# Compressing four samples' caches ahead, and two pairs of samples' attention beside the prompt's

## The chip, the core and the metric

The kernel runs on one core of a Trainium2 chip. Five engines with queues of their own work side by side: TensorE (PE) does the matrix products, VectorE (DVE), ScalarE (ACT) and GpSimd (POOL) the elementwise work, SyncE (SP) starts transfers. Each engine takes its instructions strictly in the order of its queue; an instruction whose inputs are not ready holds up everything behind it on that engine. GpSimd also starts transfers: the gathers, which fetch rows named by a list of indices. The metric is the device time of one execution, 3109.91 us before (median of 3 runs, 3104.84 to 3112.84 us).

## What is computed

One inference step of a two-layer decoder for a prompt of 512 tokens and 8 samples of one token each, in fp32. Every layer is a half-step SwiGLU, a mixer of three branches (an S5 state space, the attention NSA, a short convolution), and another half-step SwiGLU. The change is inside NSA. For a sample with 2048 earlier tokens, NSA does three things with its cache:

```python
def nsa_compress(x_raw, pe, w1, w2):      # 2048 cached rows -> 127 compressed keys and values
    ...
    h = jax.nn.gelu(h_a[:, :-1] + h_b[:, 1:] + h_pe)
    return h @ w2

# nsa_core, cut: kc, vc are the compressed keys and values
p_c = masked_softmax(s_c, ...)            # s_c = q . kc
o_c = p_c @ vc                            # branch 1: compressed
imp = p_c.sum(3) @ cmp_to_sel_map         # which blocks of 64 rows matter
score, idx = ...top_k(imp, 16)            # branch 2: the 16 best blocks
o_s = softmax(q . ks_sel) @ vs_sel
o_w = softmax(q . kw) @ vw                # branch 3: the last 512 rows
o = g[...,0]*o_c + g[...,1]*o_s + g[...,2]*o_w
```

A sample's attention therefore needs its compressed keys and values first. The prompt has the same three branches over its own 512 tokens, and does not depend on the samples.

## The kernel before

Every fp32 product of the layers' weights is three products of split operands (L239 to L241). These fill most of the time; the change touches the stretch between them in which `mid(l)` does the samples' compression and the attention. It is passed once in each layer, around 494 to 767 us and around 2000 to 2306 us of the span.

- **Compression of one sample** (`compress_cache`, L708 the products, 96 of them; `second`, L730 to L740, a gelu on ScalarE, six small products and the elementwise ends that make `kcT` and `vc`). Its raw pages come over SP's queue (L641) into `cx` (even samples, one buffer) or `raw` (odd samples, two buffers). It is a generator that yields `None` after each sample, so `upto(C, 2)` runs it two samples further.
- **Attention of a pair of samples** (`samples(l, g)`, g = 0 to 3, called S0 to S3 here): compressed scores L1138, the choice of blocks, scores of the selected pages L1189, of the window L1198, values of the pages L1249 and of the window L1258, compressed values L1264, and the end L1273. All eight pages of each half are multiplied and masked, so `sg` holds whole pages: of the 32 pages of a pair 12 come by gathers which GpSimd starts (L1118) and 20 by SP (L1122). Pair g+1 is asked for in the code right after the values of pair g (its `sag` pool holds one pair only), and the window rows `W` follow (L1127).
- **The prompt's attention** (`prompt_attention`, a generator of heads, three branches in each of four tiles of 128 tokens). A head is two scores (L1048 to L1050), a maximum on VectorE (L1051), an exponential on ScalarE (L1052), transposes (L1060), their copies, and values (L1072). After the fourth head of a branch come a reciprocal (L1077), a multiply that spreads the gates over the heads (L1079, on GpSimd, its result is `over`), a product of `over` that brings it into a score bank (L1098, the "correction" below), and the multiply and add of L1101 to L1103 (the add on GpSimd).

`weave` takes steps from several generators by their estimated cost in ns; that fixes the order of the program, from which a scheduler makes the order of each engine's queue. Before, two samples are compressed alone; S0, S1 and S2 are woven each with the compression of two further samples; S3 is woven with the prompt's attention, whose remaining heads then run alone. While S3 lives, the prompt's values have one bank (`paY`), afterwards two (`last`).

Of the kernel before, what the change touches and what calls it, by code (L numbers as in the profile page):

```python
# [122 lines left out]
class Trunk:  # L123
# [376 lines left out]
    def mid(self, l):  # L500
        nc, I = self.nc, self.I
        right, att = self.right, ExitStack()
        keep = self.pool(right, "keepb", side="right")
        self.ysam = keep.tile([128, 4, NS], F32, name="ysam")
        a = self.pool(att, "att", side="right")
        self.rows = a.tile([128, 4, 512], F32, name="rows")
        self.srows = a.tile([NS, 512], F32, name="srows")
        self.qT = a.tile([128, 4, 512], F32, name="qT")
        self.ks = a.tile([128, 2, 2, 512], F32R, name="ks")
        self.kTs = a.tile([128, 2, NS], F32, name="kTs")  # L510
        self.QB = a.tile([128, NS, 32], F32, name="QB")
        self.gtok = a.tile([128, 4, 24], F32, name="gtok")
        self.gat = a.tile([128, 4, 3], F32, name="gat")
        self.kcp = a.tile([128, 2, 32], F32, name="kcp")
        self.vcp = a.tile([128, 4, 2, 64], F32, name="vcp")
        self.w2 = a.tile([128, 2, 64], F32, name="w2")
        self.w2r = a.tile([128, 64], F32, name="w2r")
        self.hpe = a.tile([128, 2], F32, name="hpe")
        kcv, sag = self.pool(att, "kcv", 2, side="right"), self.pool(att, "sag", 4, side="right")
        sw = self.pool(att, "sw", 2, side="right")  # L520
        self.sgq = []
        sb = ExitStack()
        self.open_banks(4, 2)
        self.saT = self.psum(sb, "saT", 2, "right")
        cxs = ExitStack()
        with ExitStack() as sf, ExitStack() as sc:
            cx, G = self.project_kvq(l, cxs, sc, self.pool(sf, "ft", 4, side="right"), sag, sw)
        self.banks.close()
        self.saM, self.saS = (self.psum(sb, n, k, "right") for n, k in (("saM", 1), ("saS", 2)))
        with ExitStack() as sc, ExitStack() as pb:  # L530
            self.cacc, self.ctp = self.psum(pb, "cacc", 2), self.psum(pb, "ctp", 1)
            cp = self.pool(sc, "cmp")
            with ExitStack() as s0:
                C = self.compress_cache(l, cp, kcv, cx, G, self.compress_start(l, self.pool(s0, "cp")))
                self.finish(self.upto(C, 2))
            sa = self.pool(att, "sa", side="right")
            S = [self.samples(l, g, sa, sag, sw) for g in range(4)]
            for g in range(3):
                self.weave(self.slow(S[g]), self.upto(C, 2))
        cxs.close()  # L540
        ybs = ExitStack()
        self.yb = self.pool(ybs, "yb").tile([128, 4, 512], F32, name="yb")
        with ExitStack() as sc, ExitStack() as pb:
            self.paS, self.paY = self.psum(pb, "paS", 2), self.psum(pb, "paY", 1)
            self.score_banks, self.value_banks = [self.paS, self.saS], [self.paY]
            self.weave(self.last(S[3]), self.prompt_attention(l, self.pool(sc, "pa", 3)))
        att.close()
        sb.close()
        self.open_banks(4, 4)
        kc = self.pool(right, "keepc", side="right")  # L550
        self.yc = [kc.tile([128, 4, NTOK], F32R, name=f"yc{i}") for i in range(2)]
        ybh, ybl = (kc.tile([128, 4, NTOK], F32R, name=n) for n in ("ybh", "ybl"))
        for src, g, c in [(self.ysam, slice(0, 4), slice(0, NS))] + \
                [(self.yb[:, g:g + 1], slice(g, g + 1), slice(NS, NTOK)) for g in range(4)]:
            nc.scalar.activation(ybh[:, g, c], src, AF.Copy)
            nc.vector.tensor_sub(ybl[:, g, c], src, ybh[:, g, c].bitcast(F32))
        ybs.close()
        mg1, mg2 = self.pool(right, "mg1", side="right"), self.pool(right, "mg2", 2, side="right")
        left = ExitStack()
        self.ya = self.pool(left, "keepya").tile([128, 4, NTOK], F32, name="ya")  # L560
        sc, sr = ExitStack(), ExitStack()
        s5 = self.s5(l, self.pool(sc, "s5"), self.pool(sc, "s52", 2))
        conv = self.conv(l, self.pool(sr, "cv"), self.pool(sr, "cv2", 2), self.pool(sr, "cw", 2))
        merge = self.merge(l, mg1, mg2, (ybh, ybl))
        over = []

        def first():
            yield from s5
            yield from self.until(lambda: over)
            sc.close()  # L570
            kg = self.pool(right, "keepa", side="right")
            self.yg = [kg.tile([128, 4, NTOK], F32R, name=f"yg{i}") for i in range(2)]
            yield from self.glu(l, self.pool(left, "glu"), self.pool(left, "glu2", 2))

        def second():
            yield from conv
            sr.close()
            over.append(True)
            yield from self.upto(merge, 1)

        self.weave(first(), second())
        left.close()
        self.open_banks()
        mg = self.pool(right, "mg", side="right")
        self.mh = mg.tile([128, KD, NTOK], F32R, name="mh")
        self.ml = mg.tile([128, KD, NTOK], F32R, name="ml")
        self.open_res()
        for k in range(KD):
            for a, b in HALF:
                nc.gpsimd.tensor_add(self.xf[:, k, a:b], self.xh[:, k, a:b].bitcast(F32), self.xl[:, k, a:b].bitcast(F32))  # L590
        self.finish(merge)
        self.set_next(self.pairs(I["w_o"][l], 4))
        self.project_out(l, self.mh, self.ml, self.ffn_tiles(I["ffn2_w_gu"][l]))
        right.close()
# [69 lines left out]
    def compress_cache(self, l, p, kcv, cx, G, start):  # L664
# [47 lines left out]
        def second(b, acc):  # L712
            if b % 2 == 0:
                self.kcT = kcv.tile([128, 2, 128], F32, name="kcT")
                self.vc = kcv.tile([128, 2, 128], F32, name="vc")
            kcT, vc = self.kcT[:, b % 2], self.vc[:, b % 2]
            h = p.tile([128, 4, 128], F32, name="hc")
            nc.vector.memset(h[:, :, 127:128], 0.0)
# [13 lines left out]
            pa = self.bank(self.ctp)  # L732
# [30 lines left out]
        for b in range(NS):  # L763
            acc = [self.bank(self.cacc) for _ in range(1 if b else 2)]
            if b + 1 < NS:
                N = self.fetch_cmp(l, b + 1, cx)
            for s in range(8):
                if s < 7:
                    prepare(b, G, s + 1)
                elif b + 1 < NS:  # L770
                    G = N
                    prepare(b + 1, G, 0)
                products(b, acc, s)
                yield 1720.0
            yield from second(b, acc)
            yield None
# [353 lines left out]
    def samples(self, l, g, p, pg, pw):  # L1130

        nc = self.nc
        G = self.sgq[g]
        QB, kcT, vc = self.QB, self.kcT, self.vc
        M = self.bank(self.saM)

        for j in range(2):
# [48 lines left out]
        for c in range(2):  # L1186
            S = self.bank(self.saS)
# [6 lines left out]
        S = self.bank(self.saS)  # L1194
# [760 lines left out]
```

## Time and profile before

| quantity | value |
|---|---|
| median of 3 runs | 3109.91 us (3104.84 to 3112.84) |
| the profiled execution | 3104.94 us |
| its span | 3103.2 us |
| TensorE busy | 98% |
| GpSimd busy | 17% |
| granted clock of TensorE over the span | 0.987 |
| S2 beside the compression of two samples, layer 0 and 1 | 45.6 and 42.9 us |
| S3 beside the prompt's attention, layer 0 and 1 | 48.4 and 48.4 us |

The span leaves out 1.7 us around it. A share of busy time is a mean over all stages: a wait is looked for in the stretch in which it stands, and there the row's idle time before an instruction names what ended it. The granted clock is the share of TensorE's full 2.4 GHz that was allowed; 0.5 is its lower level of 1.2 GHz.

### The profile page before, as it was taken

Reading aid. Unit: us, or ns where it says so; the run is one execution under the profiler, and the core shown is the slowest. Engines: PE = TensorE matmul, PEld = TensorE weight load, DVE = VectorE, ACT = ScalarE, POOL = GpSimd, SP = SyncE. Lnnn points to the kernel's source line nnn. Section 1 sums busy time; section 2 is a strip of 40 time slices with the busy share of each in tenths; the row PEclk is TensorE's granted clock in tenths of the full one; section 3 lists DMA queues with packets and bytes.
Section 4 is the critical chain, followed back from the end, with each engine's and each line's share of the span. In section 5 each row is a group of like instructions: output and inputs, shape, how many; then the busy total and the mean of one; then the engine's idle time right before and its main releaser. Section 6 shows DMA issues by size and latency. Waiting matters only on the chain. (4 is left out here: it accounts for less than half of the span.)

```text
span 3103.2 us, 62136 instructions
## 1 busy us (share of the span) xinstructions
PE 3028.1 (98%) x25364; PEld 2906.8 (94%) x25364; DVE 1598.7 (52%) x3586; ACT 1120.1 (36%) x2226; POOL 536.1 (17%) x809
## 2 busy tenths in 40 slices
PE   8999999999999999999999999999999999999998
PEld 8999998777999999999999999887789999999998
DVE  7633356566655365333496333565666453743334
ACT  4332235456224233232233222354652242333322
POOL 2611031321001021001147010213210010210010
PEclk9999999999999999999999999999999999999999
DMA  5543254632553232232234332547234433223221
GB/s 159 198 148 133 89 159 134 209 96 63 156 138 103 88 101 91 82 99 86 82 121 169 96 103 76 172 124 218 83 93 140 122 98 102 89 82 103 89 87 64
DMA packets 358630, 360.17 MB, mean 116 GB/s; under 512 B 40068, under 2 KB 341668, under 8 KB 358216
## 3 DMA queue, kind: packets, MB, share of 16 engines
q1 hardware_dynamic: 342584, 333.58, 34.4%
q0 software_dynamic: 7440, 20.00, 2.2%
q8 instruction: 199, 3.26, 0.4%
q10 hardware_dynamic: 8320, 2.62, 0.4%
q14 instruction: 87, 0.71, 0.1%
HBM read 332.48 MB, written 36.28 MB: 119 GB/s over the span
## 5 line engine op out<-in xcount | busy, mean ns | idle before, releaser
L239 PE MATMUL ps<-xh,whi 128*128 128x264 f32 (+1 forms) x4448 | 1257.6, 285 | 14.1 <-ACT whi L228 6.1
L240 PE MATMUL ps<-xl,whi 128*128 128x264 f32 (+1 forms) x4448 | 1257.4, 284 | 2.0 <-DVE xl L323 2.0
L241 PE MATMUL ps<-xh,wlo 128*128 128x264 f32 (+1 forms) x4448 | 1254.1, 283 | 2.4 <-DVE wlo L229 2.4
L229 DVE TENSOR_TENSOR wlo<-raw,whi 128x1024 fp32r<-128x1024 f32 (+3 forms) x432 | 496.0, 1151 | 741.2 <-ACT whi L228 736.9
L239 PEld LDWEIGHTS ps<-xh,whi 128*128 128x128 f32 x4448 | 837.2, 189 | 18.7 <-ACT whi L228 6.9
L240 PEld LDWEIGHTS ps<-xl,whi 128*128 128x128 f32 x4448 | 839.5, 189 | 3.5 <-DVE xl L323 2.2
L241 PEld LDWEIGHTS ps<-xh,wlo 128*128 128x128 f32 x4448 | 838.5, 189 | 4.1 <-DVE wlo L229 3.6
L228 ACT ACTIVATE whi<-raw 128x1024 fp32r<-128x1024 f32 (+2 forms) x452 | 444.6, 988 | 891.0 <-PE ps L240 776.4
L240 PE MATMUL ps<-hl,whi 128*128 128x256 f32 (+1 forms) x1408 | 398.3, 283 | 0.0
L239 PE MATMUL ps<-hh,whi 128*128 128x256 f32 (+1 forms) x1408 | 398.2, 283 | 0.0
L241 PE MATMUL ps<-hh,wlo 128*128 128x256 f32 (+1 forms) x1408 | 398.1, 283 | 0.0
L241 PEld LDWEIGHTS ps<-hh,wlo 128*128 128x128 f32 x1408 | 265.3, 188 | 0.2
L239 PEld LDWEIGHTS ps<-hh,whi 128*128 128x128 f32 x1408 | 264.9, 188 | 0.3
L240 PEld LDWEIGHTS ps<-hl,whi 128*128 128x128 f32 x1408 | 264.8, 188 | 0.1
L260 POOL TENSOR_TENSOR xf<-xf,shift 128x264 f32<-128x264 f32 (+1 forms) x84 | 79.4, 983 | 1028.6 <-ACT shift L257 1028.6
L384 DVE TENSOR_TENSOR s<-s,ps 128x264 f32<-128x264 f32 (+1 forms) x176 | 74.3, 424 | 277.3 <-PE ps L241 277.0
L708 PE MATMUL ps<-xc,whi 128*128 128x256 f32 (+1 forms) x1024 | 167.4, 297 | 1.0 <-ACT xc L693 0.9
L385 ACT ACTIVATE hh<-s 128x264 fp32r<-128x264 f32 (+1 forms) x176 | 72.7, 415 | 245.2 <-DVE s L384 245.1
L708 PEld LDWEIGHTS ps<-xc,whi 128*128 128x128 f32 x1024 | 142.2, 193 | 14.6 <-issue 7.7
L1118 POOL DMA_INDIRECT sg<-in_selT_dram,idx x96 | 96.2, 1002 | 275.9 <-PE ps L1249 248.7
L382 ACT ACTIVATE s<-ps 128x264 f32<-128x264 f32 (+1 forms) x176 | 66.3, 379 | 128.7 <-PE ps L241 126.5
L386 DVE TENSOR_TENSOR hl<-s,hh 128x264 fp32r<-128x264 f32 (+1 forms) x176 | 76.5, 436 | 33.5 <-ACT hh L385 33.5
(471 smaller groups left out, 4206.8 us busy)
## 6 DMA issues: line engine op xcount, KB each, us to landing
raw<-in_ffn_w_gu_dram SPq DMA_DIRECT2D x86, 1024.0 KB, 5.3
raw<-in_w_in_dram SPq DMA_DIRECT2D x38, 1024.0 KB, 5.4
raw<-in_ffn_w_down_dram SPq DMA_DIRECT2D x32, 1024.0 KB, 4.9
sg<-in_selT_dram SPq DMA_DIRECT2D x160, 128.0 KB, 3.1
cx<-in_cmpT_dram SPq DMA_DIRECT2D x128, 128.0 KB, 2.2
raw<-in_cmpT_dram SPq DMA_DIRECT2D x128, 128.0 KB, 2.5
raw<-in_ffn_w_down_dram SPq DMA_DIRECT2D x16, 768.0 KB, 4.3
W<-in_winT_dram SPq DMA_DIRECT2D x16, 512.0 KB
```

Source lines behind the costliest of these rows:

```text
L228: self.copy = self.nc.scalar.activation(hi, raw, AF.Copy)
L229: self.lo.tensor_sub(lo, raw, hi.bitcast(F32))
L239: nc.tensor.matmul(o, hi[:, k], rh, start=start and k == 0, stop=False)
L240: nc.tensor.matmul(o, hi[:, k], rl, start=False, stop=False)
L241: nc.tensor.matmul(o, lo[:, k], rh, start=False, stop=stop and k == nk - 1)
L260: nc.gpsimd.tensor_sub(self.xf[:, g, a:b], self.xf[:, g, a:b], sc[:, :n])
L382: nc.scalar.activation(s[:, :n], g, AF.Silu)
L384: nc.vector.tensor_mul(s[:, :n], s[:, :n], u)
L385: nc.scalar.activation(hh[:, j, a:b], s[:, :n], AF.Copy)
L386: nc.vector.tensor_sub(hl[:, j, a:b], s[:, :n], hh[:, j, a:b].bitcast(F32))
L708: nc.tensor.matmul(o, w[:, 2 * qq + q2, :], x[:, 2 * q2:2 * q2 + 2, z:z + n], start=not b and s < 2 and q2 + z + m == 0, stop=s > 5 and q2 ...
L1118: nc.gpsimd.indirect_dma_start(out=t[:, k], out_offset=None, in_=flat, in_offset=bass.IndirectOffsetOnAxis(ap=self.idx[:, l, b, z, k:k + 1 ...
```

## The change

Four samples are compressed alone. S0 and S1 are woven each with two further samples. S2 and S3, one after the other, are woven with the prompt's attention. So that compressed keys and values can be kept longer, their pool gets a third buffer, and each pair's are kept in a list from which `samples` takes its own.

```diff
--- before.py
+++ after.py
@@ -516,9 +516,9 @@
         self.w2 = a.tile([128, 2, 64], F32, name="w2")
         self.w2r = a.tile([128, 64], F32, name="w2r")
         self.hpe = a.tile([128, 2], F32, name="hpe")
-        kcv, sag = self.pool(att, "kcv", 2, side="right"), self.pool(att, "sag", 4, side="right")
+        kcv, sag = self.pool(att, "kcv", 3, side="right"), self.pool(att, "sag", 4, side="right")
         sw = self.pool(att, "sw", 2, side="right")
-        self.sgq = []
+        self.sgq, self.kcq = [], []
         sb = ExitStack()
         self.open_banks(4, 2)
         self.saT = self.psum(sb, "saT", 2, "right")
@@ -532,10 +532,10 @@
             cp = self.pool(sc, "cmp")
             with ExitStack() as s0:
                 C = self.compress_cache(l, cp, kcv, cx, G, self.compress_start(l, self.pool(s0, "cp")))
-                self.finish(self.upto(C, 2))
+                self.finish(self.upto(C, 4))
             sa = self.pool(att, "sa", side="right")
             S = [self.samples(l, g, sa, sag, sw) for g in range(4)]
-            for g in range(3):
+            for g in range(2):
                 self.weave(self.slow(S[g]), self.upto(C, 2))
         cxs.close()
         ybs = ExitStack()
@@ -543,7 +543,7 @@
         with ExitStack() as sc, ExitStack() as pb:
             self.paS, self.paY = self.psum(pb, "paS", 2), self.psum(pb, "paY", 1)
             self.score_banks, self.value_banks = [self.paS, self.saS], [self.paY]
-            self.weave(self.last(S[3]), self.prompt_attention(l, self.pool(sc, "pa", 3)))
+            self.weave(self.last(self.chain(S[2], S[3])), self.prompt_attention(l, self.pool(sc, "pa", 3)))
         att.close()
         sb.close()
         self.open_banks(4, 4)
@@ -713,6 +713,7 @@
             if b % 2 == 0:
                 self.kcT = kcv.tile([128, 2, 128], F32, name="kcT")
                 self.vc = kcv.tile([128, 2, 128], F32, name="vc")
+                self.kcq.append((self.kcT, self.vc))
             kcT, vc = self.kcT[:, b % 2], self.vc[:, b % 2]
             h = p.tile([128, 4, 128], F32, name="hc")
             nc.vector.memset(h[:, :, 127:128], 0.0)
@@ -1131,7 +1132,7 @@
 
         nc = self.nc
         G = self.sgq[g]
-        QB, kcT, vc = self.QB, self.kcT, self.vc
+        QB, (kcT, vc) = self.QB, self.kcq[g]
         M = self.bank(self.saM)
 
         for j in range(2):
```

Lines of the changed kernel stand one lower than before from L717 on (L1079 is L1080 there, L1098 is L1099, L1118 is L1119, L1249 is L1250). Each engine has the same instructions in both kernels, but for 8 fewer loads of a function table on ScalarE. They stand in another order.

GpSimd's queue in layer 0 before, from the first pair's gathers to the third multiply (`sg` are gathered pages, `pc` is `over`, `yb` the prompt's sum):

```order
L1118 DMA sg<-in_selT_dram,idx 128x256 x12
L229 TENSOR_TENSOR wlo<-raw,whi 128x1024 x4
L1118 DMA sg<-in_selT_dram,idx 128x256 x36
L1079 TENSOR_TENSOR pc<-ps,gtok 128x512
L1103 TENSOR_TENSOR yb<-yb,pw 128x4x128
L1079 TENSOR_TENSOR pc<-ps,gtok 128x512
L1103 TENSOR_TENSOR yb<-yb,pw 128x4x128
L1079 TENSOR_TENSOR pc<-ps,gtok 128x512
```

The same place in the changed kernel:

```order
L1119 DMA sg<-in_selT_dram,idx 128x256 x12
L229 TENSOR_TENSOR wlo<-raw,whi 128x1024 x4
L1119 DMA sg<-in_selT_dram,idx 128x256 x24
L1080 TENSOR_TENSOR pc<-ps,gtok 128x512
L1104 TENSOR_TENSOR yb<-yb,pw 128x4x128
L1080 TENSOR_TENSOR pc<-ps,gtok 128x512
L1104 TENSOR_TENSOR yb<-yb,pw 128x4x128
L1119 DMA sg<-in_selT_dram,idx 128x256 x12
L1080 TENSOR_TENSOR pc<-ps,gtok 128x512
L1104 TENSOR_TENSOR yb<-yb,pw 128x4x128
```

The last 12 gathers, those of the fourth pair, stood ahead of the first multiply; now they stand between the second and the third.

TensorE's queue in layer 0 before, at the third correction (`ps<-cst,pc`), from the last of the pair's rows on:

```order
L1072 MATMUL ps<-wlo,rows 64x128
L1060 MATMUL ps<-cst,whi 128x128 x2
L1072 MATMUL ps<-wlo,rows 64x128 x4
L1273 MATMUL ps<-cst,OS 128x64
L1072 MATMUL ps<-wlo,rows 64x128 x3
L1098 MATMUL ps<-cst,pc 128x128 x4
L1048 MATMUL ps<-ks,raw 128x256
```

In the changed kernel, the 12 rows up to the third correction (L1139 is the fourth pair's compressed scores):

```order
L1050 MATMUL ps<-ks,raw 128x256
L1051 LDWEIGHTS identb
L1051 MATMUL ps<-masks,identb 128x128
L1139 MATMUL ps<-kcT,QB 32x127 x2
L1061 MATMUL ps<-cst,whi 128x128 x4
L1049 MATMUL ps<-ks,raw 128x256
L1050 MATMUL ps<-ks,raw 128x256
L1051 LDWEIGHTS identb
L1051 MATMUL ps<-masks,identb 128x128
L1061 MATMUL ps<-cst,whi 128x128 x2
L1049 MATMUL ps<-ks,raw 128x256
L1099 MATMUL ps<-cst,pc 128x128 x4
```

Between the end of the pair before (the `OS` product) with the values that follow it and this correction there are now two groups of scores with six transposes, half of a third group, and the first two products of the fourth pair.

## Rows read from the trace of the kernel before

**Rows 1.** The page, part 1: busy time, share, instructions.
```profile
PE 3028.1 (98%) x25364; PEld 2906.8 (94%) x25364; DVE 1598.7 (52%) x3586; ACT 1120.1 (36%) x2226; POOL 536.1 (17%) x809
```

**Rows 2.** Busy time and clock of both layers' stages (columns: core 0's line).
```profile
core 0: us, PE busy (x) PEld busy (x) DVE busy (x) ACT busy (x) POOL busy (x), PEclk, DMA share, GB/s
516.50:528.80 12.30, 12.30 (x105) 11.85 (x104) 6.60 (x20) 6.00 (x15) 0.00 (x0) 1.00 0.41 120
607.00:652.60 45.60, 42.89 (x372) 34.92 (x372) 23.87 (x72) 24.28 (x51) 11.59 (x12) 0.93 0.52 159
652.60:701.00 48.40, 44.90 (x400) 33.04 (x398) 32.81 (x111) 29.09 (x95) 12.90 (x17) 0.93 0.28 87
701.00:766.60 65.60, 64.25 (x587) 50.20 (x587) 44.07 (x92) 42.77 (x113) 10.55 (x9) 1.00 0.12 31
2149.10:2192.00 42.90, 40.64 (x373) 32.42 (x372) 23.81 (x72) 24.23 (x51) 11.62 (x12) 1.00 0.53 169
2192.00:2240.40 48.40, 44.93 (x399) 33.02 (x398) 32.74 (x111) 29.06 (x95) 12.85 (x17) 0.93 0.30 92
```

**Rows 3.** TensorE's waits beside the third pair in layer 1.
```profile
engine line waited for: us in total, times, longest us
PE ps L1189 <- DMA sg<-in_selT_dram,idx: 1.2, 1, 1.2
PE ps L736 <- ACT hc L730: 1.0, 1, 1.0
```

**Rows 4.** Line groups: the keys of layer 1's third pair, then its fourth.
```profile
L1189 PE MATMUL ps<-sg,QB 128*32 128x512 f32 x16 | 4.3, 601 | 1.2 <-DMA sg<-in_selT_dram,idx 1.2
...
L1189 PE MATMUL ps<-sg,QB 128*32 128x512 f32 x16 | 1.9, 598 | 0.0
```

**Rows 5.** Busy time of the half-clock stretch beside layer 0's third pair.
```profile
629.80:636.70 6.90, 6.08 (x27) 5.77 (x28) 3.46 (x13) 4.27 (x9) 0.00 (x0) 0.51 0.00 0
```

**Rows 6.** TensorE's timeline, layer 0, the end of the third pair's values.
```profile
start us, us, engine line op out<-in xcount [idle before <-releaser]
644.52 1.08 PE L1249 MATMUL ps<-sg,PT 128*32 128x128 f32 x32
645.53 0.74 PE L708 MATMUL ps<-xc,whi 128*128 128x256 f32 x4
```

**Rows 7.** GpSimd's timeline, layer 0: first and last gather, third multiply.
```profile
645.85 0.94 POOL L1118 DMA_INDIRECT sg<-in_selT_dram,idx  x1 [30.93 <-PE ps L1249]
...
660.20 0.95 POOL L1118 DMA_INDIRECT sg<-in_selT_dram,idx  x1 [0.31 <-issue]
...
696.82 1.04 POOL L1079 TENSOR_TENSOR pc<-ps,gtok 128x512 f32<-128x512 f32 x1 [9.17 <-DVE ps L1077]
```

**Rows 8.** TensorE's timeline, layer 0, prompt attention around the third correction.
```profile
694.77 0.38 PE L1048 MATMUL ps<-ks,raw 128*128 128x256 f32 x1
...
697.84 0.38 PE L1048 MATMUL ps<-ks,raw 128*128 128x256 f32 x1
...
698.40 0.36 PE L1048 MATMUL ps<-ks,raw 128*128 128x256 f32 x1
...
701.67 0.71 PE L1098 MATMUL ps<-cst,pc 128*128 128x128 f32 x4
```

**Rows 9.** TensorE's timeline: a pair's two compressed scores.
```profile
607.02 0.38 PE L1138 MATMUL ps<-kcT,QB 128*32 128x127 f32 x2
```

**Rows 10.** TensorE's timeline: a wait ahead of a half-clock stretch.
```profile
408.62 0.56 PE L284 MATMUL ps<-mean,lns 128*128 128x1 f32 x2 [4.51 <-DVE lns L270]
```

**Rows 11.** Busy time and clock in two stretches of 6.2 us behind that wait.
```profile
408.60:414.80 6.20, 6.18 (x29) 6.20 (x30) 3.94 (x15) 1.44 (x3) 1.28 (x2) 0.51 0.58 180
414.80:421.00 6.20, 6.20 (x54) 6.20 (x53) 4.43 (x13) 1.61 (x4) 4.68 (x6) 1.00 0.29 85
```

**Rows 12.** The gathers' issues, 480 to 700 us (last column: median us to landing).
```profile
sg<-in_selT_dram,idx POOLq DMA_INDIRECT x36, 3.9
```

## Prediction

> **What bounds the kernel now.** I read the page first, then the busy time stage by stage, then TensorE's waits in the stages that the change touches, and last the timelines of TensorE and GpSimd there. TensorE is busy for 98% of the span, GpSimd for 17% [rows 1]. So a microsecond counts where TensorE waits or runs at its lower clock, and an engine with much idle time can still matter if one of its instructions comes late. By stages [rows 2]: two samples' compression alone has no gap (12.30 of 12.30 us busy in layer 0's stretch of it). S2 beside the compression leaves TensorE idle for 45.60 − 42.89 = 2.7 us in layer 0, 42.90 − 40.64 = 2.3 in layer 1. S3 beside the prompt leaves 3.5 in each layer, the prompt alone 65.60 − 64.25 = 1.35. TensorE runs the same multiset of matmuls after the change as before, so the sum is over gaps, slow stretches and overlaps alone.
>
> **What goes: S2 beside compression.** In layer 1 that stage loses 2.3 us to gaps, and its 16 key products cost 4.3 us where the fourth pair's, whose pages had long landed, cost 1.9 [rows 4]: 2.4 more, though the same shapes at the same mean of some 600 ns. Keys that come page by page are issued in pieces and don't overlap each other. Together 4.7, of which I take 4.6. The waits that I can name are keys on their gather, 1.2, and a gelu, 1.0 [rows 3]. Layer 0's same stage is 45.6 − 42.9 = 2.7 us longer, because 6.9 us of it ran at a clock of 0.51 [rows 5]; that is 4.6 + 2.7 = 7.3. In the changed kernel S2's pages are asked for at the end of S1, as now, and the compression that took S2's cover is done alone, where nothing gaps. Gain: 7.3 + 4.6 = 12 us. It is 5 us if only the gaps go, 13 at most. S1's weave has the same work beside it as now and keeps its gaps: I count nothing.
>
> **What comes: GpSimd's third multiply behind 12 gathers.** This is the step on which the forecast rests. The fourth pair's 12 gathers begin when the third pair's last value product L1249 has ended, because both use the same buffers: the products from 644.52 on are followed by the next at 645.53 [rows 6], the first gather starts at 645.85. The last ends at 660.20 + 0.95 = 661.15, 15.3 us later [rows 7]. Before, GpSimd had nothing else to do meanwhile, and the third multiply came at 696.82 after 9.17 us of idle time [rows 7]. In the changed kernel the third multiply, 1.04 us long, stands right behind those gathers in an in-order queue, as the order above shows, and TensorE's third correction behind the multiply.
>
> Call T the end of the pair's last L1249. The gathers end at T + 0.3 + 15.3, and `over` is there at T + 17.0 with the multiply and a gap of 0.3. When does TensorE come to the correction? Before, beside S3, the third correction began at 701.67 and S3's last L1249 had ended where the row at 694.77 follows it: 6.9 us [rows 8]. The rows now moved ahead of it are two groups of scores with six transposes, a score product and the two compressed scores. A group with two transposes takes 698.40 − 697.84 = 0.56 [rows 8], so two take 1.1; two more transposes and the single product about 0.5, an estimate from the same rows; the compressed scores 0.38 [rows 9]. Together 2.0 to 2.1. TensorE arrives at T + 9.0 and waits for 8.0 us per layer. No row before shows this wait. From below: 6.5, if the rows in between run with gaps of their own. From above: 9.0, if they overlap better. Two layers: +16. Queued behind the correction on TensorE is everything else, the rest of the prompt's heads and S3. S3's keys need the same gathers at about T + 20 with the pages of SP, and the wait pushes TensorE past that point, so they add no second one.
>
> By the Trainium skill, "DMA: Bandwidth & Descriptors", section "Issuing engines are not separate DMA queues", the time that a sequencer takes to initiate a DMA "is usually small relative to the DMA itself". By that rule the multiply would hardly be late, and the time would be rival C's 3099 us. The rows differ: 12 issues occupy GpSimd for 15.3 us, 1.25 each, while one gather lands 3.9 us (median) after its issue [rows 7, 12].
>
> **The clock behind that wait.** A wait of 4.51 us elsewhere was followed by a stretch at a granted 0.51, the 1.2 GHz level [rows 10, 11]: 29 matmuls in 6.2 us where the next 6.2 us, at full clock, took 54. That lost 6.2 × (1 − 29/54) = 2.9 us. An 8 us wait is longer; but S3's stage already has such a stretch now (its clock is 0.93 over 48.4 us [rows 2]), and the new one may replace it rather than add. From 0 to 2.9 per layer; I take 2.2, +4.4 for both.
>
> **The rest.** S2 now runs beside the prompt as S3 did. That stage has 3.5 us of gaps per layer; some of it belongs to its start and to the last sample's gelu, and doesn't repeat, and 1.35 of the prompt's own gaps get covered. On the other side, one value bank serves the prompt for twice as long, and the fourth pair's prompt heads stand among fewer of S3's rows. Between −3 and +5; I take +2. The loads of function tables on ScalarE that go away lie beside busy TensorE: nothing. The third buffer of the compressed keys takes no time.
>
> **Sum**, on the profiled execution: 3104.94 − 12 + 16 + 4.4 + 2 = 3115.3 us. That execution lies 5.0 us under the median 3109.91, on which the forecast is to be read: 3120 us, 10 more than before. With the ends of the terms it runs from −13 + 13 + 0 − 3 = −3 to −5 + 18 + 5.8 + 5 = +24. Not all ends meet; for this case itself I take 3112 to 3128.
>
> **Rivals.**
>
> A. The wait is there, but costs no more than itself: the clock does not fall again, and VectorE and ScalarE get ahead during it, so that the short waits of that stage go. −12 + 16 + 0 − 1 = +3: 3113 us. For it: the stage already has its slow stretch. Against it: a wait of 4.5 us was enough for one [rows 10, 11].
>
> B. More comes than the one wait: the clock falls twice per layer (2 × 2 × 2.9 = 11.6), and values of the prompt wait for their one bank, 2.5 us in all beside S2 and S3, from the 3.5 of gaps that S3's stage has. −12 + 16 + 11.6 + 2.5 = +18: 3128 us. For it: S3's stage has a slow stretch and the most gaps of all [rows 2]. Against it: its rows are few per stretch and the prompt has cover enough.
>
> C. On the other side, faster. The place is GpSimd's queue: TensorE comes to the third correction only when the gathers are over. It decides at 17.0 us between the last L1249 and the correction; I count 9.0. The prompt's heads would have to be 8 us slower beside S2 than beside S3, or GpSimd free during its gathers. Then nothing is late, the 12 us are gained, and 3109.9 − 12 + 1 gives 3099 us. For it: now GpSimd waits up to 9.17 us for VectorE before a multiply [rows 7], so the multiply is not the last to be ready in every case. Against it: the rows in between are short and counted.
>
> That the change doesn't do what it says would be a rival if the compression alone lost as much as the weave: layer 0's 12.30 of 12.30 us speaks against it, and it has the same pages to wait for.
>
> **How the numbers follow.** The forecast has 0.52, A 0.20, B 0.13, C 0.15. A measurement of this kernel can tell 0.3%, 9.3 us, from no change. The forecast's +10 lies at that bound: I give 0.30 of it to slower and 0.22 to the same. A (+3) is the same, B (+18) slower, C (−11) faster for 0.12 of its 0.15. Faster 0.12, the same 0.45, slower 0.43. The range of 8 in 10 reaches from C's time with a little of its spread cut off, 3100, to a little over B's, 3130.
>
> **What would show it.** In the profile after: in the prompt stage of both layers one idle stretch of TensorE of some 8 us before the third correction, put down to GpSimd's multiply; the multiply starting straight after the twelfth gather, about 16 us after the third pair's last L1249; a lower granted clock just behind; in the weaves only S0's and S1's gaps; S3's keys at 1.9 us without a wait. It would be wrong if the correction starts within 1 us of the product ahead of it (C), if TensorE waits for a value bank or for S3's keys by several us (B), or if the four samples' compression alone shows gaps on its pages.

## The result and the profile after

The changed kernel takes 3130.61 us (median of 5 runs, 3124.15 to 3132.50) against 3111.19 us before (5 runs): slower, ratio 1.006, 95% interval [1.0042, 1.0078]. The profiled execution took 3124.15 us, its span 3122.4, 19.2 more than the one before. Part 1 of its page, which answers to [rows 1]:

```profile
PE 3031.6 (97%) x25364; PEld 2916.4 (93%) x25364; DVE 1600.0 (51%) x3586; ACT 1110.9 (36%) x2218; POOL 542.0 (17%) x809
```

TensorE's busy time has hardly grown (3031.6 us, 3028.1 before): 15.7 of the 19.2 us are gaps. (Busy time is no measure of work, though: it grows where the clock falls and shrinks where products overlap.) I cut the span at the same matmuls in both traces: the first compression product of each layer, the first prompt score, the prompt's last matmul, the last of all.

| stretch | before, us | after, us | difference |
|---|---|---|---|
| start to layer 0's first compression product | 493.94 | 503.67 | +9.7 |
| layer 0, compression and its weaves | 158.68 | 139.00 | −19.7 |
| layer 0, prompt part | 113.95 | 134.40 | +20.4 |
| from there to layer 1's first compression product | 1269.79 | 1272.33 | +2.5 |
| layer 1, compression and its weaves | 155.61 | 141.53 | −14.1 |
| layer 1, prompt part | 114.02 | 135.02 | +21.0 |
| the rest | 787.27 | 786.56 | −0.7 |

S2 has moved from the second and fifth row of this table to the third and sixth, so only the sums of the pairs tell: +0.8 in layer 0, +6.9 in layer 1. The attention, which the prediction priced at +10.4, cost 7.7. The other 11.5 us lie where nothing was edited. The attention of both layers as a whole, before (first two lines) and after:

```profile
493.94:766.57 272.63, 261.82 (x2324) 213.39 (x2323) 163.78 (x484) 154.32 (x394) 52.77 (x55) 0.97 0.39 116
2036.36:2305.99 269.63, 259.89 (x2323) 211.00 (x2323) 163.57 (x483) 153.61 (x393) 52.76 (x55) 0.98 0.39 117
503.67:777.07 273.40, 257.63 (x2323) 212.31 (x2323) 164.43 (x484) 150.29 (x390) 52.26 (x55) 0.97 0.39 116
2049.40:2325.95 276.55, 260.79 (x2323) 215.31 (x2323) 164.69 (x484) 150.18 (x390) 52.27 (x55) 0.95 0.38 114
```

TensorE's idle time grew by 5.0 us in layer 0 and 6.0 in layer 1. If half of its busy time in the stretches at the lower clock counts as lost, an estimate from these traces, the clock cost 0.2 us more than before in layer 0 and 6.6 more in layer 1. What remains of the busy time shrank by 4.4 and 5.7 us, by better overlap. So the layers differ by the clock. In layer 0 the slow stretch beside S2's compression [rows 5] is gone. Layer 1 had none there to lose, and has a new one in S1's weave (whether in every execution is not shown):

```profile
2167.90:2174.70 6.80, 5.31 (x26) 5.08 (x26) 1.53 (x4) 5.38 (x12) 0.00 (x0) 0.50 0.00 0
```

Inside the attention, busy times of core 0 (columns as in [rows 2]): compression alone, S1's weave in layer 0, the prompt parts.

```profile
core 0: us, PE busy (x) PEld busy (x) DVE busy (x) ACT busy (x) POOL busy (x), PEclk, DMA share, GB/s
503.70:560.80 57.10, 57.10 (x450) 54.09 (x449) 31.62 (x100) 28.79 (x78) 0.00 (x0) 0.98 0.43 126
598.65:642.60 43.95, 40.05 (x371) 32.56 (x371) 24.05 (x72) 25.76 (x52) 11.37 (x12) 1.00 0.55 164
642.67:777.07 134.40, 122.57 (x1142) 92.56 (x1141) 86.15 (x242) 74.73 (x217) 35.13 (x38) 0.94 0.29 88
2190.93:2325.95 135.02, 123.14 (x1142) 93.12 (x1141) 86.41 (x242) 74.61 (x217) 35.14 (x38) 0.92 0.29 85
```

Compression alone is without a gap (57.10 of 57.10). S1's weave keeps its gaps, 3.9 us (2.9 before). The prompt parts are idle for 11.8 and 11.9 us (4.9 and 4.8 before). TensorE's longest waits in layer 0's whole attention, which answer to [rows 3], and GpSimd's and TensorE's timelines, which answer to [rows 7] and [rows 8]:

```profile
engine line waited for: us in total, times, longest us
PE ps L1099 <- POOL pc L1080: 6.5, 1, 6.5
PE ps L1230 <- ACT SB L1218: 2.7, 2, 1.9
PE ps L1049 <- DVE scm L1145: 1.6, 1, 1.6
```

```profile
start us, us, engine line op out<-in xcount [idle before <-releaser]
684.10 0.98 POOL L1119 DMA_INDIRECT sg<-in_selT_dram,idx  x1 [7.44 <-PE ps L1250]
...
697.90 0.94 POOL L1119 DMA_INDIRECT sg<-in_selT_dram,idx  x1 [0.30 <-issue]
698.86 1.05 POOL L1080 TENSOR_TENSOR pc<-ps,gtok 128x512 f32<-128x512 f32 x1
```

```profile
683.78 0.38 PE L1049 MATMUL ps<-ks,raw 128*128 128x256 f32 x1
...
693.15 0.36 PE L1049 MATMUL ps<-ks,raw 128*128 128x256 f32 x1
699.96 2.08 PE L1099 MATMUL ps<-cst,pc 128*128 128x128 f32 x8 [6.45 <-POOL pc L1080]
```

The longest wait is the one that was forecast, here 6.45 us, at the third correction, put down to GpSimd's multiply. The gathers begin at 684.10, after the third pair's last values (the next row of TensorE stands at 683.78), and end at 698.84; the multiply starts at once, 698.86. TensorE issued the row ahead of the correction at 693.15 and could do nothing more till 699.96. Layer 1 has the same 6.5 us. What followed, in layer 0 and layer 1, with the next stretch of layer 0 between:

```profile
699.90:706.80 6.90, 6.84 (x30) 5.79 (x31) 2.23 (x6) 2.95 (x8) 1.28 (x2) 0.50 0.62 216
706.80:713.70 6.90, 6.90 (x71) 4.17 (x69) 5.47 (x23) 3.64 (x11) 1.04 (x1) 0.99 0.01 1
2248.10:2256.40 8.30, 8.25 (x47) 7.17 (x48) 2.84 (x8) 3.59 (x10) 1.27 (x1) 0.50 0.47 169
```

Behind the wait the clock is granted 0.50, the 1.2 GHz level: in layer 0 30 matmuls in 6.9 us, then 71 in the next 6.9, though of other shapes. S3's 16 keys in layer 0 answer to [rows 4]: 2.1 us, no wait.

```profile
L1190 PE MATMUL ps<-sg,QB 128*32 128x512 f32 x16 | 2.1, 605 | 0.0
```

Now the 9.7 us ahead of the attention. Both traces are at most 1.5 us apart up to 131 us of the span, in the middle of layer 0's first feed-forward half, and some 8 us at 144. Busy times between 131 and 144 us, before, and after with TensorE's waits:

```profile
131.00:144.00 13.00, 13.00 (x121) 12.63 (x120) 6.70 (x11) 4.44 (x11) 8.72 (x30) 1.00 0.39 155
```

```profile
131.00:144.00 13.00, 9.10 (x66) 8.45 (x65) 10.42 (x14) 7.21 (x15) 12.06 (x27) 0.74 0.49 169
```

```profile
PE ps L239 <- ACT whi L228: 2.4, 1, 2.4
PE ps L241 <- DVE wlo L229: 1.5, 1, 1.5
```

TensorE is idle for 3.9 us, and its clock falls behind that: some 7 us together. TensorE waits for a split of weights, ScalarE for the weights (`raw`), and these for SyncE's queue. SyncE between 104 and 123 us, before, then after:

```profile
start us, us, engine line op out<-in xcount [idle before <-releaser]
106.07 3.32 SPq L218 DMA_DIRECT2D raw<-in_ffn_w_gu_dram  x2
114.34 0.34 SPq L1507 DMA_DIRECT2D s5d<-room  x1
114.73 0.88 SPq L975 DMA_DIRECT2D out_win_s_dram<-in_cache_win_kv_dram  x1
```

```profile
104.17 0.89 SPq L976 DMA_DIRECT2D out_win_s_dram<-in_cache_win_kv_dram  x1
115.78 0.33 SPq L1508 DMA_DIRECT2D s5d<-room  x1
121.59 0.32 SPq L1519 DMA_DIRECT2D dk<-room  x1
122.01 7.06 SPq L218 DMA_DIRECT2D raw<-in_ffn_w_gu_dram  x2
```

Before, two weight loads (L218) go out at 106.07; after, at 122.01. Ahead of them now stand the copy of the window cache to its output (L976, L975 before) and two stores of the S5 preparation (L1508, L1519), which wait till 121.59 for their data. The copy is written at the start of the prompt's attention, over 500 us later, in both kernels; it needs nothing, so the scheduler may put it wherever SyncE is free. The change moved its place in the program ahead of S2, and the scheduler took it some 10 us earlier, ahead of the weight loads.

### The profile page after: what moved, and what is told of

The parts are those of the page before. It is cut to its first block, busy times and chain, and to the rows that moved or that the text cites. A ratio compares the mean times of both kernels' runs of the same rounds, so it can differ in the third digit from the quotient of the medians.

```text
span 3122.4 us, 62119 instructions
## 1 busy us (share of the span) xinstructions
PE 3031.6 (97%) x25364; PEld 2916.4 (93%) x25364; DVE 1600.0 (51%) x3586; ACT 1110.9 (36%) x2218; POOL 542.0 (17%) x809
## 5 line engine op out<-in xcount | busy, mean ns | idle before, releaser
L239 PE MATMUL ps<-xh,whi 128*128 128x264 f32 (+1 forms) x4448 | 1259.6, 286 | 19.2 <-ACT whi L228 11.0
L1119 POOL DMA_INDIRECT sg<-in_selT_dram,idx x96 | 94.5, 984 | 288.1 <-PE ps L1250 260.9
```

The costliest lines, as they stand in the source:

```text
L239: nc.tensor.matmul(o, hi[:, k], rh, start=start and k == 0, stop=False)
L1119: nc.gpsimd.indirect_dma_start(out=t[:, k], out_offset=None, in_=flat, in_offset=bass.IndirectOffsetOnAxis(ap=self.idx[:, l, b, z, k:k + 1 ...
```

## Experiments

Theory: the loss has two causes, the copy's new place with the order it brings to the first feed-forward half, and the third multiply behind the gathers. Rivals: the first is chance of one execution or belongs to the attention; at the second place something else would hold TensorE for as long. The chips differ: on the two chips of e1 to e4 and of f1 to f4 the kernel before takes 3195 us, and in the runs of gathers of their traces TensorE, VectorE and ScalarE stand still for long; g1 to g3 and h1 ran on a chip where it takes 3109. Each ratio is to the kernel before on its own chip. The changed kernel itself ran on the chip of the result and as f1, not beside g1 to h1; the multiply alone was moved only on chips with stalls.

**e1, the copy later**

```diff
 def prompt_attention(self, l, p):
-        self.nc.sync.dma_start(self.O["win_s"][l, :, 0:511], self.I["cache_win_kv"][l, :, 1:512])
 def samples(self, l, g, p, pg, pw):
+        if g == 3:
+            self.nc.sync.dma_start(self.O["win_s"][l, :, 0:511], self.I["cache_win_kv"][l, :, 1:512])
```

> The changed kernel, with one transfer asked for later in the code: the copy of the window cache to its output (L976), which the changed kernel asks for at the start of the prompt's attention, is asked for at the start of S3, as many samples on as in the kernel before. Theory: some 8.5 us of the 19 lost lie in layer 0's first feed-forward half, because that copy and two stores moved ahead of two weight loads on SyncE's queue; then this kernel's first compression product starts at about 494 us as in the kernel before (503.7 in the changed one), the 2.4 and 1.5 us waits near 135 us are gone, and the time is 9 to 10 us under the changed kernel's, about 3121. The 6.5 us waits on GpSimd stay. Rival: the loss near 135 us was a disturbance of that one execution or belongs to the changed attention; then the time stays within 3 us of 3130.

**e2, the kernel before with the copy earlier**

```diff
             for g in range(3):
+                if g == 2:
+                    self.nc.sync.dma_start(self.O["win_s"][l, :, 0:511], self.I["cache_win_kv"][l, :, 1:512])
 ...
-        self.nc.sync.dma_start(self.O["win_s"][l, :, 0:511], self.I["cache_win_kv"][l, :, 1:512])
```

> The kernel before, with that copy asked for ahead of S2 and nothing else changed. Theory: the first feed-forward half takes the changed kernel's order, TensorE waits for a split of weights near 135 us for some 2.4 and 1.5 us with a half-clock stretch behind it, and the kernel gets slower by 8 to 10 us, to about 3120, though its attention is that of before. Rival (the loss belongs to the changed attention): no change, 3111.

Measured: e1 1.0015 [1.0003, 1.0026], e2 1.0027 [1.0016, 1.0037]. Busy times between 131 and 144 us, e1 then e2:

```profile
131.00:144.00 13.00, 13.00 (x121) 12.64 (x120) 6.71 (x11) 4.44 (x11) 9.30 (x31) 1.00 0.37 150
```

```profile
131.00:144.00 13.00, 5.92 (x43) 4.70 (x43) 10.52 (x14) 4.96 (x9) 10.75 (x18) 0.74 0.15 60
```

The one line decides. With the copy later the changed kernel's stretch is full again, with the weight loads at 105.90; with the copy earlier the kernel before, whose attention is untouched, is idle there for 7.1 us at a clock of 0.74. All eleven traces of kernels with gathers divide the same way. In the changed kernel, e2, e3, f1 and f3, where the copy goes out first, these weight loads go out at 120.2 to 122.0 us and TensorE is busy for 5.9 to 9.4 of the 13 us; in the other six they go out at 105.8 to 107.2 and it is busy for all 13. In time e2 costs 7.2 us by the medians (3202.40 and 3195.21). e1's absolute forecasts missed, as this was not the chip of the result; its gain is read against f1 below.

**e3, the third multiply on VectorE; e4, both edits**

```diff
-            (nc.vector if t == 3 and br else nc.gpsimd).tensor_mul(over, ...
+            (nc.vector if t == 3 and br or t == 1 and not br else nc.gpsimd).tensor_mul(over, ...
```

> The changed kernel, with the third multiply alone (second tile, first branch) on VectorE in place of GpSimd. Theory: the two waits of 6.5 us at the third correction go, and with them the half-clock stretch behind each (some 3.5 and 4.2 us): 15 to 20 us less than the changed kernel, about 3111 to 3115; up to 3 us per layer may come back as a wait for the fourth pair's keys. Rival: the correction is only where the lateness shows; the fourth pair's pages or the maxima on VectorE hold TensorE next for about as long, and the gain is under 6 us, 3125 or more.

> The changed kernel with both edits: the copy asked for at S3 and the third multiply on VectorE. Theory: the two losses are independent, so the gains add, 24 to 30 us under the changed kernel: 3101 to 3107, that is 4 to 10 us under the kernel before, the first 12 us of gain that the change was worked out to have coming to light in part. Rival of the second edit: 3115 to 3119.

Measured: e3 1.0021 [1.0012, 1.0031], e4 1.0000 [0.9988, 1.0011]. Both forecasts were made for the chip of the result and missed here. From e3 to e4, 6.5 us, is the copy once more; the multiply's worth can't be read on this chip. What hides it, in e2, with the attention of before: 18 us around layer 0's second run of gathers, the same run in the kernel before on the chip of the result, and the longest wait of VectorE in e2's attention of layer 0.

```profile
574.00:592.00 18.00, 8.44 (x87) 6.41 (x76) 0.96 (x5) 0.74 (x3) 11.38 (x12) 0.79 0.63 190
```

```profile
554.30:572.30 18.00, 18.00 (x166) 14.92 (x156) 7.97 (x25) 8.99 (x16) 12.04 (x12) 1.00 0.80 238
```

```profile
DVE OS L1270 <- remote: 43.4, 3, 14.8
```

On the chip of the result TensorE is busy for 18.00 of 18 us during 12 gathers. Here it is for 8.44, VectorE for 0.96, with a wait of 14.8 us for something that the trace calls remote and puts to no engine of the core. In f1, the changed kernel on such a chip, TensorE waits 11.5 us for VectorE during the fourth pair's gathers, before it comes to the third correction:

```profile
735.37 0.66 PE L1061 MATMUL ps<-cst,whi 128*128 128x128 f32 x2 [11.51 <-DVE wlo L1065]
```

The multiply is done at 734.92 there, and no wait is put down to it.

**f1, the changed kernel again; f2, the third buffer alone; f3 and f4, as e3 and e4**

```diff
-        kcv, sag = self.pool(att, "kcv", 2, side="right"), self.pool(att, "sag", 4, side="right")
+        kcv, sag = self.pool(att, "kcv", 3, side="right"), self.pool(att, "sag", 4, side="right")
```

(f2, in the kernel before.)

> The changed kernel itself, unaltered, beside the three others on one chip. The runs e1 to e4 were on a chip where the kernel before takes 3195 us and all engines stand still for 8 to 15 us in each run of gathers, so that their times could not be set against the changed kernel's. If this chip does so too, the changed kernel takes some 3203 us, 8 over before: the first feed-forward half's loss alone, since the stall during the gathers holds TensorE longer than the late multiply. If it does not, 3130, 19 over before.

> The kernel before with the third buffer of compressed keys and nothing else; its order is that of before on TensorE, ScalarE, GpSimd and SyncE. Theory: no change, within 3 us of before. It also gives a trace of the attention of before on this chip. Rival, that the buffer's place in memory costs time: 5 us or more.

> The changed kernel with the third multiply on VectorE. Without stalls in the gathers, theory: the waits of 6.5 us at the third correction go and the slow stretch behind them, 15 to 20 us under the changed kernel, 3111 to 3115; rival, the fourth pair's pages or VectorE hold TensorE next: gain under 6 us. With stalls in the gathers: the same as the changed kernel within 3 us.

> The changed kernel with the third multiply on VectorE and the window copy asked for at S3. Without stalls, theory: 24 to 30 us under the changed kernel, 3101 to 3107, faster than before by 4 to 10 us. With stalls: 7 to 9 us under the changed kernel, level with before.

Measured: f1 1.0034 [1.0022, 1.0045], f2 0.9998 [0.9989, 1.0007], f3 1.0025 [1.0013, 1.0038], f4 1.0008 [0.9997, 1.0019]. All four as expected for a chip with stalls: the buffer is free, the changed kernel is 8.9 us slower, the multiply does little, both edits together bring it level. e1 beside f1, 1.0015 and 1.0034, makes the copy's place worth some 6 us, and f4 is 6.5 us under f3.

**g1, g2: no gathers, all pages by SyncE; g3: GpSimd filled instead**

```diff
-            for k in range(NG):
+            for k in range(0):
 ...
-            for k, s in enumerate(self.pages(src, l, b, 8 * z + NG, 8 - NG)):
-                nc.sync.dma_start(t[:, NG + k], s)
+            for k, s in enumerate(self.pages(src, l, b, 8 * z + 0, 8 - 0)):
+                nc.sync.dma_start(t[:, 0 + k], s)
```

g3 is g2 with, for pairs 1 to 3:

```diff
+            if g:
+                for k in range(4):
+                    v = t[:, 6:8].rearrange("p a f -> p (a f)")
+                    nc.gpsimd.tensor_add(v, self.fill, self.fill)
```

> The kernel before, with all 32 pages of a pair asked for by SyncE, none by a gather of GpSimd (in e1 to e4 and f1 to f4 the gathers brought stalls of all engines that hide what the change does). Theory on these stalls: they come with the gathers, so this kernel is some 60 us under the kernel before on this chip, near 3130; the keys of each pair wait longer, since SyncE's 20 pages took 14.4 us and 32 take 23. Rival: the stalls come with the pages on SyncE's queue, and the time stays or rises, 3195 or more.

> The changed kernel with all pages by SyncE. No gather stands ahead of the third multiply now, and the first feed-forward half has the order of before up to some 2000 matmuls. Theory: with the late multiply and the moved copy gone, the change gains what its compression stage gains, some 6 to 10 us per layer less 2 to 3 of the prompt's stage: 8 to 16 us under the kernel before without gathers, and no wait over 2 us at the third correction. Rival: the change costs by itself (S2 beside the prompt is no better cover than compression), within 4 us of the kernel before without gathers, or slower.

> The changed kernel with all pages by SyncE, and where the 12 gathers of a pair stood, 16 additions on GpSimd that write zeros' sums into the buffers before the pages land (4 into each of the four buffers, 128x512, 1.04 us each by the multiply of that shape: some 16.6 us of GpSimd, no transfer, the results are overwritten). Theory (it is GpSimd's occupation that makes the multiply late, whatever fills it): the wait at the third correction is back, 6 to 9 us in each layer, put down to the multiply, with a slow stretch behind it; 14 to 26 us over the changed kernel without gathers. Rival (the transfers of the gathers, their traffic or their stalls, made the wait): no such wait, within 5 us of it.

Measured, on a chip without stalls: g1 3130.14 us, 1.0064 [1.0049, 1.0080]; g2 3123.45, 1.0051 [1.0034, 1.0069]; g3 3165.68, 1.0180 [1.0158, 1.0202]. g1 meets the number 3130 for a wrong reason: here the kernel before takes 3109, and leaving out the gathers costs 21 us. So its question, whether the stalls come with the gathers, stays open. g2 is 6.7 us under g1 by the medians, a little under the 8 forecast, and has no wait at the third correction: without gathers the change gains (attention −3.9 us in layer 0, −5.2 in layer 1). That holds between these two alone: g1's own attention is 5.8 and 9.9 us longer than that of the kernel before with gathers. g2's prompt parts, layer 0 and layer 1:

```profile
651.67:781.65 129.98, 124.51 (x1142) 90.20 (x1141) 85.52 (x242) 76.06 (x218) 16.83 (x19) 0.99 0.32 92
2194.34:2324.86 130.52, 125.07 (x1142) 90.53 (x1141) 85.40 (x242) 76.08 (x218) 16.83 (x19) 0.99 0.32 91
```

They are 4.4 and 4.5 us shorter than the changed kernel's. g3, GpSimd's and TensorE's timelines at the place in layer 0, then busy times of its prompt part and of the stretch behind the wait:

```profile
698.10 16.05 POOL L1123 TENSOR_TENSOR sg<-fill 128x512 f32<-128x512 f32 x16 [7.25 <-PE ps L1252]
714.11 1.04 POOL L1082 TENSOR_TENSOR pc<-ps,gtok 128x512 f32<-128x512 f32 x1
```

```profile
715.20 2.08 PE L1101 MATMUL ps<-cst,pc 128*128 128x128 f32 x8 [7.30 <-POOL pc L1082]
```

```profile
651.72:797.28 145.56, 131.44 (x1141) 96.96 (x1141) 90.90 (x242) 75.10 (x217) 44.36 (x45) 0.91 0.29 81
715.20:722.00 6.80, 6.80 (x37) 6.01 (x39) 2.27 (x6) 3.04 (x9) 1.28 (x1) 0.50 0.76 214
```

The wait is back, 7.30 us in layer 0 and 14.6 in both, without any gather: GpSimd's occupation is enough to make it. That is what the run was for. Its size was off: 42 us over g2, not 14 to 26. The prompt part is 15.6 longer, with more slow clock (0.91), other waits, and VectorE busy for 97.0 us where the same work took 90.2 in g2. The additions also hold back the pages of the buffers that they write: SyncE waits 7.5 us for them in layer 0. How these share the rest was not taken apart.

**h1, both edits, on the chip of g1 to g3**

> The kernel of e4 and f4 once more (the changed kernel with the third multiply on VectorE and the window copy asked for at S3), for a chip without the stalls in the gathers, where the kernel before takes some 3109 us. Theory: the copy's place is worth some 8.5 us, the two waits of 6.5 us and the slow clock behind them 13 to 20: 3101 to 3109, level with the kernel before or up to 8 us under it; in the trace no wait over 2 us near 135 us of the span nor at the third correction. Rival: the fourth pair's keys or VectorE take the place of the wait, 3112 to 3121. On a chip with the stalls: level with before, 3195, as e4 and f4.

Measured: 3111.18 us (12 runs) against 3108.46, ratio 1.0007 [0.9997, 1.0016]: level with before, where the changed kernel was at 1.006 on the chip of the result. Some 17 of its 19 us are back, near the edge between theory and rival, and the trace has some of both. (Its profiled execution took 3119.91 us, the longest of the 12, so I compare stretches and not the span.) TensorE at the third correction in layer 0; then busy times near 135 us and of the prompt parts:

```profile
690.13 0.71 PE L1098 MATMUL ps<-cst,pc 128*128 128x128 f32 x4
...
701.97 1.02 PE L1191 MATMUL ps<-sg,QB 128*32 128x512 f32 x2 [2.32 <-DMA sg<-in_selT_dram,idx]
```

```profile
131.00:144.00 13.00, 13.00 (x121) 12.63 (x120) 7.52 (x12) 4.44 (x11) 7.58 (x27) 1.00 0.48 194
642.62:770.70 128.08, 120.58 (x1143) 90.07 (x1142) 88.46 (x243) 74.69 (x217) 34.72 (x37) 0.97 0.31 92
2189.21:2319.05 129.84, 121.91 (x1143) 90.45 (x1141) 88.28 (x243) 74.69 (x217) 34.73 (x37) 0.96 0.30 90
```

The stretch near 135 us is full. The correction comes at 690.13 with no wait, 9.8 us earlier than in the changed kernel, whose prompt part began at the same 642.6. But the fourth pair's keys now wait 2.3 us for their gather, and the prompt part is 6.3 us shorter in layer 0 and 5.2 in layer 1, not by the 10 or so that the wait and the slow clock behind it came to. The whole attentions are at +1.1 and −0.2 us against before, where the changed kernel's were at +0.8 and +6.9. So in layer 0 this trace shows no gain in all: its compression and weaves took 145.65 us, 6.65 more than in the changed kernel, with more slow clock (10.2 us at 0.50 in S1's weave). Whether that belongs to the kernel or to this long execution was not tested. No version that beats the kernel before was found.

## Why the prediction was right, and where it was not

- Slower was right; it had 0.43 of the chances. The median, 3130.61 us, is 0.6 us over the 3130 at which the range ends, and the ratio 1.006 on the 3109.91 from which the forecast starts gives 3128.6, inside; the 3112 to 3128 given for the case itself were passed either way. The forecast of +10 was for the attention, which cost 7.7 in the traces; the total was +19.4 by the medians. The attention's 7.7 alone lies under the 9.3 us that the prediction held to be the least that can be told from no change. So that the result is clear of it hangs on the 11.5 us that it had not priced, and is in part luck.
- **The sum left out a term.** It failed at the sentence that the same multiset of matmuls leaves "gaps, slow stretches and overlaps alone", and then looked for these in the attention only. The order of SyncE's queue in the first feed-forward half had changed too, and the prediction put no price on that. Shown by e1, e2 and the eleven traces: some 7 us, from one transfer's place in the program. The remaining 4 or so of the 11.5 us are of one to two microseconds each at several places; none was tested.
- **The attention's 7.7 beside 10.4** is in part luck. By the terms of the sum, gaps were to go by 4.6 us and the wait to add 16, +11.4; idle time grew by 11.0. The clock was to give 2.7 and cost 4.4, +1.7; it cost 6.8. The overlap of the keys was to give 4.6; overlap gave 10.1. The last two errors, each of some 5 us, met. The +2 of the rest was not forecast by kind.
- **The third multiply behind the gathers**: right. 8.0 us per layer forecast, 6.45 measured: the gathers ended 15.1 us after the values and not 15.6, and the multiply followed without the gap that I had added (ready at T + 16.1, not 17.0); TensorE came at T + 9.7 by its wait, not 9.0. That the wait costs its whole length was wrong: beside h1 it is worth 5 to 6 us of the prompt part, slow clock included, since without it the keys wait. That figure comes from traces of both edits together; the multiply alone was not timed on a chip without stalls.
- **S3's keys behind the wait**: right. They take 2.1 us without a wait after, and wait 2.3 us when the multiply is no longer late.
- **The clock**: 2.2 us per layer forecast. The slow stretch behind the wait came in both layers, 6.9 and 8.3 us of work at 0.50, half of it lost by estimate, 3.4 and 4.1 us. Layer 1 got a further one, in S1's weave, for which the sum counted nothing. Of rival B, this much was right: the clock falls more often; no wait for a value bank is among the waits of layer 0.
- **The gain of 12 us** can't be read off the table, as S2's work moved with it (−19.7 and −14.1 hold it). Its 2.7 us of slow clock went from layer 0, and a like stretch came in layer 1. Gain and cost beside the prompt together show in g2 beside g1: 9 us in the attention with nothing late, a little under the 12 − 2 that the sum had. With gathers this was not measured.
- **Rival C** asked for TensorE to come to the correction after the gathers; it came 6.45 us before the correction could start. By the rule of the Trainium skill, "DMA: Bandwidth & Descriptors", section "Issuing engines are not separate DMA queues", the time that a sequencer takes to initiate a DMA is usually small relative to the DMA itself. The trace does not agree for a run of gathers: 12 issues held GpSimd from 684.10 to 698.84 us, 1.25 each, where one gather landed 3.8 us (median, 480 to 715 us) after its issue.

## What to carry to other kernels

Where a scheduler orders the queues, compare every queue from its first instruction, not just the part that was edited: a transfer that waits for nothing can stand hundreds of microseconds ahead of its place in the program (over 500 here), and a small shift there can push weight loads back (16 us here). Work on an engine that also issues gathers is late by the whole run of gathers that stands ahead of it, however idle that engine is on average. A wait taken away is worth what is late next, not its length.

## What was not expected of the hardware

On two of the chips TensorE, VectorE and ScalarE stood still for long in the attention's runs of 12 gathers: in the run shown TensorE was busy for 8.44 of 18.00 us and VectorE for 0.96, with waits that the trace puts to no engine of the core. In the same run on the chip of the result TensorE was busy for all 18.00. The same kernel takes 3195 us there and 3109 here. That the gathers cause it was not shown, as the kernels without them ran elsewhere.
